# A hybrid retention / RWKV-7 / mixture-of-experts block: TensorE's order in the first phase written by the kernel

## The chip, the core and the metric

The kernel runs on one core of a Trainium2 chip. The metric is the device time of one execution in microseconds (us). Engines are named as the profile names them: PE is TensorE, PEld its weight loads, DVE VectorE, ACT ScalarE, POOL GpSimd, and SP the queue that issues almost all transfers.

## The reference

One layer over 2048 tokens of width 1024, in float32:

```python
xn = rms_norm(h, norm1_gain[l])
proj = xn @ w_in[l]
...
ret = jax.nn.silu(rp[..., 3 * RET_WIDTH:]) * ret.reshape(B, S, RET_WIDTH)
rw = rwkv7_time_mix(proj[..., 4 * RET_WIDTH:], ...)
mixed = jnp.concatenate([ret, rw], axis=-1).astype(x.dtype)
h = h + mixed @ w_out[l]
h = h + hier_moe(rms_norm(h, norm2_gain[l]), ...)
```

`ret` is retention with 4 heads of 128 (rotary q and k, decayed scores inside a chunk, a state from chunk to chunk, and a head norm). `rw` is the RWKV-7 recurrence with 8 heads of 64: each token's state is the old one times a decay, plus a rank-one correction, plus `v k^T`; then a head norm, a bonus term and a gate. The mixture of experts picks 2 of 32 experts for each token.

## The kernel before

**Phases.** The first phase makes `mixed`. The second multiplies it by `w_out` (tiles `wo`, `mT`, results `acc`) and routes the tokens. The third runs the experts. The first phase is what the change touches. Its work on TensorE falls into these parts.

- *Projections*, four groups of 512 tokens. `norm_a` and `norm_b` make the normalised, transposed input `nT` as a high and a low part; `rwkv_proj` makes 14 column blocks with 24 matmuls of 512 columns each (`gemm_fm`, results `pj`), and inside it `lora`; `ret_head` makes k, q, gate and v of one retention head (`gemm_fm`, `gemm_v`). Weights come chunk by chunk through `wchunk`: a transfer, a cast on ACT, a subtraction on DVE.
- *Retention cores* (`core`), 16 of them, one for each head and group: short products in `pk` (steps r0 to r4 below), then `head_center` (two reductions, a square, 12 small operations for the reciprocal root, on DVE, ACT and POOL in turn), then the transposes of L649.
- *RWKV units*, 16 of 128 tokens. `rwkv_prep` loads a unit, makes the norms (`pb` of 8 columns), transposes, and multiplies inner products (`pb<-ar,bk`: for each half of the unit two products whose weights and data lie on 64 partitions, the first on the lower 64, the second on the upper); their masked results are `pt`. POOL then solves 32x32 triangles in 31 double steps (L486, L488): `pt` goes to memory as `nl_d`, comes back as `ln`, the result goes out as `xl_d` and comes back as `t1s`. `rwkv_inv` joins the triangles to inverses (`psi`, beginning with the transpose of `t1s` at L511). `rwkv_chain` does two chunks of 64 tokens in series: `psr` (with the state `sbd`), `psz<-rs_,inv`, `psz<-uv,bkt` (new state), and two products `psz<-uv,pt` and `psr<-uv,pt` of 64x64. `rwkv_fin` centres the heads (`head_center`), transposes at L572 and applies the gate.

**What sets the order.** The program is written part by part. A scheduler places every instruction on its engine by a priority and by its own estimate of when operands will be ready; `tc.high_priority(offset=...)` raises a part (units `PRW`, `PRC`, `PRF`; weights `soon()`). Each engine then runs its list strictly in order, so an instruction that waits holds everything behind it.

## Time and profile before

| | us |
|---|---|
| three runs: median (lowest to highest) | 2427.48 (2424.75 to 2428.06) |
| the profiled execution: its time / its span | 2430.18 / 2428.4 |
| projections, 16 to 1188 us: length / TensorE busy | 1172.0 / 1088.2 |
| from the last projection to the first `acc`, 1188 to 1265 us | 77.0 / 54.2 |
| the rest of the second phase to the routing, 1265 to 1535 us | 270.0 / 266.3 |
| routing, 1535 to 1578 us | 43.0 / 21.6 |
| experts, 1578 to 2428 us | 850.4 / 776.9 |

The span runs from the first to the last instruction; the execution's own time is 1.8 us longer. A window's second number is the time in which at least one matmul was in flight. A matmul in flight overlaps the next, so the pace of a dense row of matmuls is read from the starts of consecutive rows and not from a mean duration.

### The profile page before, as it was taken

The page shows a single profiled execution, that of the slowest core. Times are in us where ns is not written, and L with a number is a line of the kernel's source. Part 1 is how long each engine was busy: PE and PEld are TensorE (multiplying, and loading weights), DVE is VectorE, ACT ScalarE, POOL GpSimd, SP SyncE. Part 2 cuts the span into 40 slices and gives each one's busy share as a digit, 9 for nine tenths or more (in the row PEclk, how much of TensorE's full clock was granted, in tenths as well). Part 3 has the DMA queues.
Part 4 walks back from the last instruction along what each step waited for, and adds up shares of the span by engine and source line. Part 5 has one row for each costly group of instructions (what it writes and reads, how often), then busy time and mean ns, then how long its engine had stood idle before and what let it go on. Part 6 is the DMA issues. An engine that isn't in the chain of part 4 may idle for free.

```text
span 2428.4 us, 36379 instructions
## 1 busy us (share of the span) xinstructions
PE 2207.2 (91%) x11816; PEld 1810.3 (75%) x11817; DVE 1710.4 (70%) x3500; ACT 1129.7 (47%) x1932; POOL 1161.3 (48%) x1530
## 2 busy tenths in 40 slices
PE   5999889998898989999879999699999999999990
PEld 4887778887787867877768888577777777777770
DVE  4477766878666877567775766768777787777875
ACT  4343433534434345333322222366666666666663
POOL 2036444354441575136542333466666666666650
PEclk9998999989999999999969999799999999999995
DMA  6643254432544335433234454488989999889978
GB/s 207 210 150 94 81 175 143 137 89 84 173 138 130 90 92 174 123 93 104 76 106 123 129 202 146 138 296 287 304 293 290 302 290 301 295 282 299 292 255 297
DMA packets 291298, 454.78 MB, mean 187 GB/s; under 512 B 93392, under 2 KB 164496, under 8 KB 291088
## 3 DMA queue, kind: packets, MB, share of 16 engines
q1 hardware_dynamic: 277136, 414.10, 51.6%
q0 software_dynamic: 13824, 37.80, 7.3%
q8 instruction: 94, 1.54, 0.3%
q14 instruction: 100, 0.82, 0.1%
q10 hardware_dynamic: 144, 0.52, 0.1%
HBM read 375.18 MB, written 81.85 MB: 188 GB/s over the span
## 4 chain that ended last, share of the span: by engine, by line
PE 47%; POOL 11%; DMA 7%; DVE 6%; issue 5%; ACT 3%; SPq 2%; POOLq 0%; DVEq 0%; ACTq 0%
PE acc L152 32%; PE pj L152 6%; POOL xl L488 5%; POOL tm L486 4%; PE pb L152 2%; PE tp L152 2%; ACT hl L913 1%; PE tp L1025 1%; DMA ln<-nl_d 1%; DVE hl L914 1%; PE psz L152 1%; DMA h_d<-yo,ti 1%; DMA xl_d<-xl 1%; PE psi L152 1%; SPq L490 1%
## 5 line engine op out<-in xcount | busy, mean ns | idle before, releaser
L152 PE MATMUL pj<-nT,whl 128*128 128x512 f32 x2496 | 626.4, 403 | 9.6 <-DVE nT L319 5.3
L914 DVE TENSOR_TENSOR hl<-raw,hl 128x1024 fp32r<-128x1024 f32 x259 | 444.1, 1745 | 142.6 <-ACT hl L913 142.6
L152 PEld LDWEIGHTS pj<-nT,whl 128*128 128x128 f32 x2496 | 464.9, 192 | 106.7 <-DVE nT L319 5.8
L152 PE MATMUL acc<-hl,xT 128*128 128x512 f32 (+1 forms) x2048 | 511.3, 402 | 0.0
L152 PEld LDWEIGHTS acc<-hl,xT 128*128 128x128 f32 (+1 forms) x2048 | 367.2, 183 | 100.8 <-ACT xT L172 0.2
L914 POOL TENSOR_TENSOR hl<-raw,hl 128x1024 fp32r<-128x1024 f32 x125 | 332.6, 2672 | 219.2 <-ACT hl L913 163.2
L913 ACT CAST hl<-raw 128x1024 fp32r<-128x1024 f32 x353 | 352.0, 1049 | 32.7 <-DMA raw<-in_wu_dram 26.9
L249 ACT CAST whl<-wraw 128x512 fp32r<-128x512 f32 x248 | 152.3, 618 | 304.8 <-PE pj L152 240.0
L250 DVE TENSOR_TENSOR whl<-wraw,whl 128x512 fp32r<-128x512 f32 x248 | 187.8, 760 | 146.1 <-ACT whl L249 141.7
L152 PE MATMUL acc<-hl,hT 128*128 128x512 f32 (+1 forms) x1024 | 249.6, 398 | 0.0
L486 POOL TENSOR_TENSOR tm<-xl,ln 128x60 f32<-128x60 f32 (+24 forms) x496 | 179.1, 361 | 105.6 <-DMA ln<-nl_d 69.0
L152 PEld LDWEIGHTS acc<-hl,hT 128*128 128x128 f32 (+1 forms) x1024 | 183.1, 181 | 51.7
L488 POOL TENSOR_TENSOR xl<-xl,tm 128x60 f32<-128x60 f32 (+24 forms) x496 | 187.5, 378 | 36.6
L152 PE MATMUL acc<-wo,mT 128*128 128x512 f32 x768 | 191.9, 401 | 0.0
L152 PEld LDWEIGHTS acc<-wo,mT 128*128 128x128 f32 x768 | 142.2, 191 | 28.5
L1147 POOL DMA_INDIRECT h_d<-yo,ti x48 | 107.5, 2239 | 53.8 <-DMA h_d<-yo,ti 40.5
L499 POOL COPY mbd<-pt 32x128 f32<-32x128 f32 x64 | 20.6, 321 | 226.5 <-DVE pt L464 199.4
L152 PE MATMUL pj<-whl,nT 128*128 128x256 f32 x768 | 118.6, 305 | 0.2 <-DVE gs L600 0.2
L152 PEld LDWEIGHTS pj<-whl,nT 128*128 128x128 f32 x768 | 105.9, 207 | 2.7 <-DVE gs L600 0.4
L464 DVE TENSOR_TENSOR pt<-pb,cst 64x512 f32<-64x512 f32 x128 | 88.0, 687 | 24.9 <-PE pb L152 23.1
L1014 POOL DMA_INDIRECT xb<-xt_d,ti x48 | 75.1, 1564 | 33.4 <-PE tp L1025 22.8
L172 ACT CAST xT<-tp 128x512 fp32r<-128x512 f32 x80 | 46.0, 589 | 80.7 <-PE tp L1025 65.7
(447 smaller groups left out, 3283.7 us busy)
## 6 DMA issues: line engine op xcount, KB each, us to landing
raw<-in_wg_dram SPq DMA_DIRECT2D x128, 512.0 KB, 4.7
raw<-in_wu_dram SPq DMA_DIRECT2D x128, 512.0 KB, 6.6
raw<-in_wd_dram SPq DMA_DIRECT2D x128, 512.0 KB, 6.7
wraw<-in_win_dram SPq DMA_DIRECT2D x208, 256.0 KB, 3.1
tr<-pf_d SPq DMA_DIRECT2D x80, 256.0 KB, 3.1
pf_d<-ev SPq DMA_DIRECT2D x52, 256.0 KB, 2.9
x<-in_xt_dram SPq DMA_DIRECT2D x32, 256.0 KB, 5.2
pf_d<-x SPq DMA_DIRECT2D x32, 256.0 KB, 4.2
```

The lines of the kernel that those rows point to most:

```text
L152: PE.matmul(o, l, r, start=start, stop=stop)
L172: SC.copy(dst_h, ps)
L249: SC.copy(hl[:, 0], raw)
L250: V.tensor_tensor(hl[:, 1], raw, hl[:, 0].bitcast(F32), op=ALU.subtract)
L464: V.tensor_tensor(pt[zs, i:i + 2, :, z ^ h], psp[h][zs].rearrange("p (f c) x -> p f c x", f=2), maskp[zs, None, None, :].to_broadcast([64, ...
L486: GP.tensor_tensor(tv, xl[:, 0:r, t:t + 1].to_broadcast([128, r, n]), ln[:, t:t + 1, t + 1:32].to_broadcast([128, r, n]), op=ALU.mult)
L488: GP.tensor_tensor(xl[:, 0:r, t + 1:32], xl[:, 0:r, t + 1:32], tv, op=ALU.add)
L490: SY.dma_start(xl_d[u].rearrange("l (r q) t -> q l r t", q=4)[q], xl[q * 32:(q + 1) * 32])
L913: (SC.copy if hi is SC else hi.tensor_copy)(hl[:, 0], raw)
L914: lo.tensor_tensor(hl[:, 1], raw, hl[:, 0].bitcast(F32), op=ALU.subtract)
L1014: return GP.indirect_dma_start(out=xbs[b], out_offset=None, in_=xt_d, in_offset=bass.IndirectOffsetOnAxis(ap=ti[b][:, e:e + 1], axis=0), b ...
L1147: GP.indirect_dma_start(out=h_d, out_offset=bass.IndirectOffsetOnAxis(ap=idx, axis=0), in_=y, in_offset=None, bounds_check=S + 127, comput ...
```

## The change

The first phase becomes six generators ("streams"): chains, inverses, preparations, fins, cores, projections. A clock `NOW` counts the TensorE time of what has been issued, from a formula on shape and type (0.227 for a 512-column projection matmul). `done(...)` notes it under a name in `AT`; `yield after(LAT[...], ...)` says that the stream may go on when `NOW` has come that many us past the noted point. A loop takes, at each step, the first stream in the list that may go on; if none may, it moves `NOW` ahead. TensorE's instructions stay in the order so made (`manual_schedule`); the other engines' order is still the scheduler's. Units start at least `PC_US` = 66 us apart, but for the last four.

```diff
+LAT = {"proj": 8, "load": 9, "pss": 3.5, "psi": 1.5, "bk": 11, "psp": 4.5, "pst": 1.5, "solve": 40, "i1": 1.5, "i2": 3, "inv": 3,
+       "c1": 2.5, "c2": 2.2, "c3": 3, "c4": 2, "hc": 14, "psn": 3.5, "head": 3, "r0": 2, "r1": 2.5, "r2": 4, "r3": 2, "r4": 15}
+PC_US = 66.0
...
+    NOW = [0.0]
+
     def mm(o, l, r, start=True, stop=True):
+        n = math.prod(r.shape[1:])
+        NOW[0] += max(0.107, n * 0.000443) if r.dtype == F32R else 2 * max(0.057 if r.shape[0] <= 64 else 0.107, n * 0.00088)
         PE.matmul(o, l, r, start=start, stop=stop)
+
+    def flip(o, i, ident_):
+        NOW[0] += 0.11
+        PE.transpose(o, i, ident_)
...
+        AT, INF, LOCK = {}, 1e9, [None]
+
+        def done(*k):
+            AT[k] = NOW[0]
+
+        def after(lag, *keys):
+            return lambda: max(AT.get(k, INF) for k in keys) + lag
...
         def gemm_fm(i, nT):
             ps = pj.tile([128, 512], F32, name="pj")
             for kh in range(2):
                 hl = wchunk(A["win"][i, :, kh * 512:(kh + 1) * 512])
                 for k in range(4):
+                    yield
...
+            done("load", u)
+            yield after(LAT["load"], ("load", u))
...
+            done("pss", u)
+            yield lambda: max(AT["pss", u] + LAT["pss"], AT.get(("chain", u - 2), INF if u > 1 else 0.0),
+                              AT.get(("fin", u - 3), INF if u > 2 else 0.0), PACE(u))
+            ar = rp.tile([128, 4, 2, 128], F32, name="ar", bufs=2)
...
-            psb = pb.tile([128, 4, 128], F32, name="pb")
-            mm(psb.rearrange("p f t -> p (f t)"), blk2, rt)
-            V.tensor_tensor(bon, psb, f3(vt), op=ALU.mult)
+            done("psi", u)
+            yield after(LAT["psi"], ("psi", u))
...
+            done("psv", u)
+            yield after(LAT["bk"], ("psi", u))
...
-                pst = pb.tile([128, 2, 2, 128], F32, name="pb")
-                for q in range(4):
-                    PE.transpose(pst[:, q % 2, q // 2], bk[:, i * 2 + q], ident)
-                SC.copy(bkt[:, :, i * 128:(i + 2) * 128], pst.rearrange("p c f x -> p c (f x)"))
-
+                done("psp", u, i)
+                yield after(LAT["psp"], ("psp", u, i))
...
+            done("solve", u)
+            for i in range(0, 4, 2):
+                pst = pb.tile([128, 2, 2, 128], F32, name="pb")
+                for q in range(4):
+                    flip(pst[:, q % 2, q // 2], bk[:, i * 2 + q], ident)
+                SC.copy(bkt[:, :, i * 128:(i + 2) * 128], pst.rearrange("p c f x -> p c (f x)"))
+                done("pst", u, i)
+                yield after(LAT["pst"], ("pst", u, i))
+            psb = pb.tile([128, 4, 128], F32, name="pb")
+            mm(psb.rearrange("p f t -> p (f t)"), blk2, rt)
+            V.tensor_tensor(bon, psb, f3(vt), op=ALU.mult)
+            done("prep", u)
...
+            yield lambda: INF if LOCK[0] else AT["solve", u] + LAT["solve"]
+            LOCK[0] = u
...
+            yield lambda: max(AT.get(("pst", u, 2), INF) + LAT["pst"], AT.get(("fin", u - 2), INF if u > 1 else 0.0))
...
+                done("c1", u, c)
+                yield lambda: max(AT["c1", u, c] + LAT["c1"], AT.get(("inv", u), INF) + LAT["inv"])
...
+                done("c2", u, c)
+                yield after(LAT["c2"], ("c2", u, c))
...
-            head_center(yt, 8, 64, 64e-5, py.tile([128, 512], F32, name="psi"))
+            head_center(yt, 8, 64, 64e-5, sm.tile([128, 512], F32, name="sqf", bufs=1))
+            done("hc", u)
+            yield lambda: INF if LOCK[0] is not None else AT["hc", u] + LAT["hc"]
...
+                if h == 3 and g + 1 < NG:
+                    norm_b(g + 1)
...
-            head_center(y, 4, 128, 1e-5, pk.tile([128, 512], F32, name=pkn))
-            psn = pk.tile([128, 512], F32, name=pkn)
+            head_center(y, 4, 128, 1e-5, pkb.tile([128, 512], F32, name="pk"))
+            done("r", j, 4)
...
+        def PACE(u):
+            return AT["proj", 0] + PC_US * u if u < NU - 4 else 0.0
...
+        streams = [(each(rwkv_chain, NU), PRC), (each(rwkv_inv, NU), PRC), (each(rwkv_prep, NU), PRW),
+                   (each(rwkv_fin, NU), PRF), (each(core, 4 * NG), PRO), (projections(), None)]
+        with tc.manual_schedule(engines={mybir.EngineType.PE}):
+            ready = [next(s) for s, _ in streams]
+            while any(s for s, _ in streams):
+                times = [(r() if callable(r) else 0.0 if s else INF) if s else INF for (s, _), r in zip(streams, ready)]
+                if min(times) >= INF:
+                    raise RuntimeError(f"no stream can go on: {AT}")
+                NOW[0] = max(NOW[0], min(times))
+                i = next(i for i, t in enumerate(times) if t <= NOW[0])
+                s, pri = streams[i]
+                with (tc.high_priority(offset=pri) if pri else ExitStack()):
+                    try:
+                        ready[i] = next(s)
+                    except StopIteration:
+                        streams[i] = (None, None)
     ga.close()
```

The rest of the diff puts `done` and `yield after` with the lags of `LAT` behind every further step (c3, c4, i1 to i2, psn, r0 to r3), splits `norm_b` so that its scaling is issued ahead of the group's last gate product, moves a scratch tile of the fin from PSUM to SBUF and gives the last core the same PSUM pool as the others. The number of instructions and their shapes stay as they are.

Three places in TensorE's order, before and after. First the inner products of unit 7 (`pb<-ar,bk`; the numbers tell the two results of a half apart). Before:

```order
L152 MATMUL pb_5070<-ar_4987,bk_5040 128x128 x4
L152 MATMUL pk_6376<-vtm_6032,rc_6356 128x128 x4
L152 MATMUL pj_6810<-nT3_6434,whl_6813 128x512 x3
L152 MATMUL pj_6810<-nT4_6438,whl_6830 128x512 x3
L152 MATMUL pj_6810<-nT5_6442,whl_6830 128x512 x3
L152 MATMUL pj_6810<-nT6_6446,whl_6830 128x512 x3
L152 MATMUL pj_6810<-nT7_6450,whl_6830 128x512 x3
L152 MATMUL pj_6851<-nT0_6422,whl_6854 128x512 x2
L511 MATMUL psi_4844<-cst_119,t1s_4833 128x128
L152 MATMUL pj_6851<-nT0_6422,whl_6854 128x512
L152 MATMUL pj_6851<-nT1_6426,whl_6854 128x512 x3
L152 MATMUL pb_5071<-ar_4987,bk_5040 128x128 x4
```

After:

```order
L160 MATMUL pb_6683<-ar_6551,bk_6568 128x128
L160 MATMUL pb_6684<-ar_6551,bk_6568 128x128
L160 MATMUL pb_6683<-ar_6551,bk_6568 128x128
L160 MATMUL pb_6684<-ar_6551,bk_6568 128x128
L160 MATMUL pb_6683<-ar_6551,bk_6568 128x128
L160 MATMUL pb_6684<-ar_6551,bk_6568 128x128
L160 MATMUL pb_6683<-ar_6551,bk_6568 128x128
L160 MATMUL pb_6684<-ar_6551,bk_6568 128x128
L160 MATMUL psz_6697<-uv_5753,bkt_5752 128x128 x4
```

The two products of a half stood 4 to a row with other work between them; now they alternate, one on the lower 64 partitions and one on the upper. It is so in all 32 halves (before, one half alternates throughout and a few for some rows), and in the same way the two 64x64 products of all 32 chunks alternate, which none did.

Second, the first chunk of unit 7's chain, from the product with the inverse (`psz<-rs_`) to the new state (`psz<-uv,bkt`). Before:

```order
L152 MATMUL psz_7387<-rs__7382,inv1_148 128x64 x4
L152 MATMUL pb_7180<-ar_7097,bk_7150 128x128 x4
L152 MATMUL pj_8659<-whl_8691,nT3_6434 128x256 x3
L152 MATMUL pj_8658<-whl_8720,nT4_6438 128x256 x3
L152 MATMUL pj_8658<-whl_8720,nT5_6442 128x256 x3
L152 MATMUL pj_8658<-whl_8720,nT4_6438 128x256 x3
L152 MATMUL pj_8658<-whl_8720,nT5_6442 128x256 x3
L152 MATMUL pj_8659<-whl_8720,nT4_6438 128x256 x3
L152 MATMUL pj_8659<-whl_8720,nT5_6442 128x256 x3
L152 MATMUL psz_7394<-uv_4990,bkt_4989 128x128 x4
```

After:

```order
L160 MATMUL psz_7384<-rs__6975,inv1_148 128x64 x4
L164 MATMUL pb_7391<-cst_119,tr_7199 128x128 x4
L160 MATMUL pj_7315<-whl_7381,nT2_5706 128x256 x3
L160 MATMUL pj_7315<-whl_7381,nT3_5709 128x256 x3
L160 MATMUL pj_7315<-whl_7381,nT2_5706 128x256 x3
L160 MATMUL pj_7315<-whl_7381,nT3_5709 128x256 x3
L160 MATMUL pj_7316<-whl_7381,nT2_5706 128x256 x3
L160 MATMUL pj_7316<-whl_7381,nT3_5709 128x256 x3
L160 MATMUL psz_7420<-uv_6554,bkt_6553 128x128 x4
```

There were 21 projection matmuls of 256 columns and a group of four inner products between the two; now there are 18 matmuls and four transposes.

Third, the end of the phase. Before, the last rows ahead of the first `acc`:

```order
L572 MATMUL psi_10903<-cst_119,yt_10572 128x128 x4
L152 MATMUL psi_10912<-lg_8180,lw_135 128x128 x4
L152 MATMUL psr_11309<-uv_10646,pt_10644 64x64 x4
L152 MATMUL psr_11320<-uv_10646,pt_10644 128x128 x4
L152 MATMUL psr_11320<-sbd_143,ar_10643 128x128 x4
L649 MATMUL pj_12887<-cst_119,rc_12854 128x128 x4
L152 MATMUL psz_11333<-rs__11329,inv1_148 128x64 x4
L152 MATMUL pb_11430<-tr_11371,cst_119 128x512
L447 MATMUL pb_11433<-cst_119,tr_11372 128x128 x4
L152 MATMUL acc_13059<-wo7_12982,mT_13049 128x512
```

After:

```order
L160 MATMUL psi_12496<-lg_11141,lw_135 128x128 x4
L164 MATMUL psi_12503<-cst_119,t1s_12222 128x128
L160 MATMUL pb_12506<-ar_12421,bk_12438 128x128
L160 MATMUL pb_12507<-ar_12421,bk_12438 128x128
L160 MATMUL pb_12506<-ar_12421,bk_12438 128x128
L160 MATMUL pb_12507<-ar_12421,bk_12438 128x128
L160 MATMUL pb_12506<-ar_12421,bk_12438 128x128
L160 MATMUL pb_12507<-ar_12421,bk_12438 128x128
L160 MATMUL pb_12506<-ar_12421,bk_12438 128x128
L160 MATMUL pb_12507<-ar_12421,bk_12438 128x128
L160 MATMUL psi_12503<-t1s_12222,mbd_151 128x32 x4
L160 MATMUL acc_13062<-wo7_12985,mT_13052 128x512
```

Before, the first `acc` stood behind a part of unit 15's preparation and 19 rows ahead of unit 14's inverse; now it stands behind the inner products of unit 15 and behind the first two steps of unit 14's inverse (`psi<-cst,t1s`, `psi<-t1s,mbd`). The last projection row stands 56 rows above it.

## Rows read from the trace of the kernel before

**Rows 1.** The page: span, TensorE's busy time, and its two strips of 40 slices.
```profile
span 2428.4 us, 36379 instructions
PE 2207.2 (91%) x11816; PEld 1810.3 (75%) x11817; DVE 1710.4 (70%) x3500; ACT 1129.7 (47%) x1932; POOL 1161.3 (48%) x1530
...
PE   5999889998898989999879999699999999999990
...
PEclk9998999989999999999969999799999999999995
```
**Rows 2.** Windows by stage: length, busy time of each engine, granted clock, DMA share.
```profile
16.00:1188.00 1172.00, 1088.22 (x6293) 919.01 (x6293) 827.58 (x1881) 467.59 (x954) 493.70 (x1043) 0.96 0.42 126
1188.00:1265.00 77.00, 54.19 (x297) 47.34 (x296) 57.87 (x152) 28.73 (x61) 42.97 (x97) 0.68 0.37 106
1265.00:1535.00 270.00, 266.31 (x1546) 227.79 (x1544) 167.69 (x679) 74.91 (x177) 94.29 (x151) 0.99 0.47 147
1535.00:1578.00 43.00, 21.55 (x99) 17.56 (x100) 29.53 (x119) 14.87 (x19) 16.62 (x13) 0.64 0.43 141
1578.00:2428.40 850.40, 776.90 (x3587) 598.65 (x3585) 624.31 (x650) 537.13 (x705) 508.77 (x216) 0.96 0.89 292
```
**Rows 3.** Waits of TensorE, 0 to 1500 us: total, times, longest.
```profile
PE psi L511 <- DMA t1s<-xl_d: 42.4, 16, 4.8
...
PE pk L152 <- ACT rc L621: 8.9, 3, 4.9
PE pb L152 <- DVE tr L441: 6.7, 7, 1.8
...
PE pj L152 <- ACT x L339: 4.8, 10, 1.4
...
PE pk L649 <- POOL rc L379: 3.9, 2, 3.4
...
PE psz L152 <- ACT uv L546: 0.8, 1, 0.8
```
**Rows 4.** Timeline of one solve (unit 4): start, length, engine, line, operation.
```profile
457.88 1.38 DVE L464 TENSOR_TENSOR pt<-pb,cst 64x512 f32<-64x512 f32 x2
459.29 0.80 SPq L474 DMA_DIRECT2D nl_d<-pt  x2
461.34 1.71 SPq L481 DMA_DIRECT2D ln<-nl_d  x4
465.64 0.24 POOL L486 TENSOR_TENSOR tm<-xl,ln 128x31 f32<-128x31 f32 x1 [5.70 <-DMA ln<-nl_d]
...
501.12 0.21 POOL L488 TENSOR_TENSOR xl<-xl,tm 128x8 f32<-128x8 f32 x1
501.35 2.52 SPq L490 DMA_DIRECT2D xl_d<-xl  x4
505.24 1.95 SPq L503 DMA_DIRECT2D t1s<-xl_d  x4
508.67 0.30 PE L511 MATMUL psi<-cst,t1s 128*128 128x128 f32 x1 [2.11 <-DMA t1s<-xl_d]
```
**Rows 5.** Windows around the end of that solve.
```profile
504.00:509.00 5.00, 2.89 (x18) 2.36 (x16) 3.46 (x4) 1.10 (x2) 1.56 (x1) 1.00 0.26 40
509.00:523.00 14.00, 14.00 (x64) 13.33 (x65) 5.05 (x10) 1.68 (x4) 1.14 (x4) 0.51 0.38 103
```
**Rows 6.** The chain that ended last: a stretch of 512-column matmuls without a wait.
```profile
1411.05 11.92 PE acc L152 x52
```
**Rows 7.** Timeline of TensorE: inner products of 64 rows, apart and interleaved.
```profile
764.96 1.16 PE L152 MATMUL pb<-ar,bk 64*128 64x128 f32 x8
766.05 2.18 PE L152 MATMUL pj<-whl,nT 128*128 128x256 f32 x16
...
775.17 1.16 PE L152 MATMUL pb<-ar,bk 64*128 64x128 f32 x16
776.26 1.16 PE L152 MATMUL pk<-qT,kT 128*128 128x128 f32 x8
...
1204.40 0.68 PE L152 MATMUL psr<-uv,pt 64*64 64x64 f32 x8
1205.00 1.16 PE L152 MATMUL pk<-rc,qT 128*128 128x128 f32 x8
1206.09 0.68 PE L152 MATMUL psz<-uv,pt 64*64 64x64 f32 x8
1206.69 1.16 PE L152 MATMUL psr<-uv,pt 128*128 128x128 f32 x8
```
**Rows 8.** Timeline of TensorE: last projection, an inverse, first output product.
```profile
1186.30 2.08 PE L152 MATMUL pj<-nT,whl 128*128 128x512 f32 x8
...
1214.33 0.45 PE L511 MATMUL psi<-cst,t1s 128*128 128x128 f32 x1 [3.61 <-DMA t1s<-xl_d]
...
1265.31 3.29 PE L152 MATMUL acc<-wo,mT 128*128 128x512 f32 x10
```
**Rows 9.** Timeline: a chunk's second product, and the ends of two head-centre steps.
```profile
462.99 1.08 PE L152 MATMUL psz<-rs__4237,inv 128*128 128x64 f32 x8
464.11 0.42 DVE L545 COPY uv<-psz 64x256 f32<-64x256 f32 x1 [0.54 <-PE psz L152]
464.56 0.37 ACT L546 COPY uv<-psz 64x256 f32<-64x256 f32 x1 [0.28 <-DVE uv L545]
...
468.75 1.05 PE L152 MATMUL psz<-uv,bkt 128*128 128x128 f32 x8
...
478.61 1.16 PE L152 MATMUL pk<-vtm,rc 128*128 128x128 f32 x8
...
499.67 1.49 POOL L379 TENSOR_TENSOR rc<-rc,rs_y 128x512 f32<-128x512 f32 x1
...
1240.76 1.91 PE L152 MATMUL pj<-vtm,rc 128*128 128x128 f32 x8
...
1258.37 1.04 POOL L379 TENSOR_TENSOR rc<-rc,rs_y 128x512 f32<-128x512 f32 x1
```

201 lines of the change are left out of this document (114 added, 87 removed).

## The prediction

> **What bounds the kernel now.** I read the page first, then the kernel by stages, then who waited for whom on the engine that is busiest. TensorE has something in flight for 91% of the span, and its strip stays at 8 or 9 but for two dents [rows 1]. The stages tell where the rest lies [rows 2]. In the projections, 16 to 1188 us, matmuls are in flight for 1088 of 1172 us: 84 us are idle. The granted clock there is 0.96, so about 0.04 x 1172 = 47 us of full-speed work are lost as well. In the stretch from the last projection to the first output product, 54 of 77 us are busy, at a clock of 0.68. The rest of the second phase is dense (266 of 270). Routing and experts, 893 us, are not touched.
>
> Nearly half of the idle time is one wait: the transpose that begins a unit's inverse waits for `t1s`, 16 times, 42.4 us together, 4.8 at most [rows 3]. Unit 4 shows what is behind it: the last masked product is done at 459.3, the triangles go to memory and come back, POOL solves from 465.6 to 501.3, the result goes out and comes back, and the transpose starts at 508.7 [rows 4]. That is 49 us, in which only rows of other work keep TensorE busy. [...] So TensorE is the bound of the first phase, and order alone can win back at most some 84 + 47 us there, and part of the 77.
>
> **The change, part by part.** All counts are of rows in the order, with paces from the trace: 0.229 us for a projection matmul of 512 columns (52 in 11.92 us) [rows 6], about 1.0 us for a group of four short float32 matmuls, and 0.6 us for the four of 64x64 [rows 7].
>
> *Pairs.* Four inner products on one half of the partitions, 8 passes, take 1.09 us to the next instruction (764.96 to 766.05). The one place where the two halves alternate has 16 passes in the same 1.09 us (775.17 to 776.26) [rows 7]. The change alternates all 32, of which one did: 31 x 1.09 = 34 us; I take 33 for those that did so in part. It lies on TensorE's path, nothing hides it. For the 64x64 products no alternating place exists. Apart, 8 passes take 0.60 us (1204.40 to 1205.00), 0.075 each [rows 7]; the alternating inner products run at 0.068 a pass, and at that pace 16 passes take 1.09 instead of 1.20: 32 x 0.11 = 4 us, which I take because it is the nearest row. If they overlapped fully it would be 32 x 0.60 = 19, if not at all 0. [...]
>
> *The inverse's distance.* Between the last inner product of unit 7 and its inverse stood 136 projection matmuls (31 us), six groups of short matmuls (6) and a few transposes and small ones (2): 39 us. Now there are 156 (36), seven groups (7) and 3 more: 46. Over units 0 to 13 the same count gives 42 us on average before and 46 after. The mean wait was 42.4 / 16 = 2.65 us, less than the 4 us that are added. But time between passes faster if the clock stays up and pairs overlap, and the solve itself has no reason to be quicker. I take 25 of the 42 us; the ends are 0 and 42.
>
> *The clock.* If most inverses no longer wait, most of the drops that follow them go too. Of the 47 us I take 20, less than the share of the waits, since other waits may bring the clock down; ends 0 and 47.
>
> *The end of the phase.* From the last projection to the first output product stood 32 us of rows in 77 us. Now there are 21 us of rows, but the first output product is queued behind unit 14's inverse, and that unit's inner products end only 4 us of rows ahead of the last projection. By unit 4 [rows 4], 50 us lie between the products and the inverse, so the first output product starts 50 - 4 + 2 = 48 us or so after the last projection. Rows not covered: 77 - 32 = 45 before, 48 - 21 = 27 after; with the weights of the output product loading in that time too I take 16 of the 18. Ends: 0 and 25. In [rows 8] the inverse of unit 13 stands in the middle of that stretch and waits 3.6.
>
> *Small things.* The bonus product moves from before to behind the solve, so its operand is old when it comes: it waited 6.7 us in 7 waits. Other streams go between the `lora` products, which waited 4.8 for ACT [rows 3]. I take 8 of 11.5. What else moves costs nothing while its lead lasts: the transposes of `bk` with their copies on ACT go behind the solve's transfers, the load of `lg` goes behind the norms and, in SP's list, behind the unit's other loads, and `norm_b`'s eight multiplications go ahead of a gate product. Their users (the new state, the fin's gate, the next group) stand ten us of rows or more behind them; without that lead each would be a wait of a few us once in a unit or group.
>
> *What it adds.* The scheduler left more room behind short steps than the lags do. From the product with the inverse to the new state the median was 5.0 us of rows and is now 2.5. In the trace the copies between them were done 0.9 us after the product's end, with 4.7 us until the next (464.07, 464.93, 468.75) [rows 9], so 2.5 is enough there, unless DVE is late; the row of `uv` in [rows 3] shows 0.8 us in all. The tight place is a core's head centring: 19 us of rows before, 16 after. In the trace it took from 479.8 to 501.2, 21.4 us, in one core, and from 1242.7 to 1259.4, 16.7 us, in another [rows 9]; before, the transposes waited only 3.9 us for it in all [rows 3], as other delays fell into the same 19 us. By these two the shortfall is 1 to 5.5 us in each of 16 cores, 16 to 88. A fin's head centring, with 16 us now where some 90 stood, can fall short in the same way. Behind such a transpose the whole list of TensorE waits, projections too. I take 55 for all of them, as waits elsewhere in the same 16 us cover part; ends 15 and 90.
>
> Sum: -33 - 4 - 25 - 20 - 16 - 8 + 55 = -51. The profiled execution took 2430.2, its span 2428.4 [rows 1]; 2430.2 - 51 = 2379. The median of the runs was 2.7 below the profiled execution, so I predict 2376.
>
> **The rivals.**
>
> *Slower: head centring becomes the wait that the inverse was.* Every core falls short by the 5.5 us of the slower row, 88 us, and each such wait brings the clock down as in [rows 5]: at the 47 / 16 = 3 us that a unit loses now, 48 us more, and nothing of the 20 is won. -33 - 4 - 25 - 16 - 8 + 88 + 48 = +50: 2478. It decides from a mean wait of some 4 us with such a clock, or 6.6 without. For it: 21.4 against 16, and that its DVE operations stand at low priority. Against it: waits share their time, and the same arithmetic for the order before would give waits that [rows 3] doesn't show. [...] Here the trace shows a fall after a single wait [rows 5], and no run here shows yet what many short ones do.
>
> *No change: the inverse waits as long as before.* POOL's list is still the scheduler's; if it puts rope and fin work among the solve's steps, the solve grows by what the distance has grown. Already now the last step of unit 4's solve came behind a head-centre product of POOL (499.67, then 501.12) [rows 4, 9]. Without the 25 and the 20: -6, 2421.
>
> *Much faster: the lags fit.* The head centrings cost 15, inverses and clock give back 40 each, the end of the phase 20: -37 - 40 - 40 - 20 - 10 + 15 = -132, 2295. For it: the short steps have the room that [rows 9] asks.
>
> **How the numbers follow.** The forecast has a chance of 0.50 (its own range 2345 to 2405), much faster 0.15, no gain 0.13, slower 0.22. A measurement of this kernel can tell about 0.2%, 5 us. Faster: 0.50 + 0.15 + half of the third = 0.71; same 0.07; slower 0.22. The range that leaves out 2 in 10, half of the best case and the far part of the slower one: 2310 to 2455.
>
> **What would show it.** The alternating inner products stand as rows of 16 passes with 1.1 us to the next instruction. The total of waits for `t1s` falls below 20 us. The clock of the projection window is 0.98 or more. The window from the last projection to the first output product is near 50 us. Waits for POOL's head-centre products at the two transposes total 30 to 60 us. The prediction is wrong if those pass 90, if the waits for `t1s` stay above 35, or if the projections are held by something that has no row here, as late weights.

## The result, and the profile after

The changed kernel takes 2492.4 us (median of 4 runs, 2489.8 to 2498.5) against 2427.8 before: a ratio of 1.0266, interval 1.0236 to 1.0296. I had forecast 2376. The profiled execution took 2498.5, its span 2496.8.

The page's span, TensorE's busy time and its two strips, to be read beside [rows 1]:

```profile
span 2496.8 us, 36285 instructions
...
PE 2171.8 (87%) x11816; PEld 1780.9 (71%) x11817; DVE 1719.3 (69%) x3500; ACT 1133.7 (45%) x1932; POOL 1136.2 (46%) x1530
...
PE   5998789886898887898967999699999999999990
...
PEclk9999889999899998899987999799999999999995
```

TensorE is busy for 35 us less in a span that is 68 us longer, and the clock's strip has 8s where it had 9s. The windows by stage (last projection now at 1284, first output product at 1345, last at 1594), with the columns of [rows 2]:

```profile
16.00:1284.00 1268.00, 1092.22 (x6489) 923.51 (x6490) 867.44 (x1979) 482.54 (x981) 486.02 (x1087) 0.92 0.40 119
1284.00:1345.00 61.00, 29.23 (x202) 25.16 (x200) 42.66 (x106) 21.67 (x43) 32.49 (x72) 0.69 0.40 115
1345.00:1594.00 249.00, 248.04 (x1437) 213.16 (x1436) 149.88 (x615) 67.95 (x159) 85.25 (x128) 0.99 0.49 153
```

Against [rows 2] the projections take 96 us more, the stretch to the first output product 16 less, the output products 21 less; what follows takes 903 us against 893, which stays unexplained (this execution was the longest of the four). A part of that is work that changed its place: 196 more matmuls stand in the first window and 204 fewer in the two behind it. Over all three together it is 59 us more.

The loss lies in the projections. TensorE is idle there for 176 of 1268 us (84 of 1172 before). By the clock's own records in the two traces it is busy for 152 us (76 before) at a granted share of 0.5. In such a stretch of the changed kernel's trace six projection matmuls of 512 columns take 2.71 us (1118.81 to 1121.52), 0.45 each, where 512-column matmuls take 0.229 in [rows 6]; so I put the loss at half of those times, 76 us (38 before). That is 92 + 38 = 130 us more. It came to 96, although more matmuls stand there, since the rows themselves got shorter: 1092 - 76 = 1016 us of full-speed work against 1088 - 38 = 1050. (One minus the clock of the row, times the length, gives more, 101 against 47, because it also counts time in which TensorE was idle; the prediction's 47 was read so.)

Who ended TensorE's waits, 0 to 1600 us, as in [rows 3] (total, times, longest):

```profile
PE psr L160 <- DVE yt L624: 30.3, 16, 7.7
PE pk L160 <- DVE srt L730: 27.4, 7, 6.7
PE pk L164 <- POOL rc L410: 25.1, 6, 7.1
PE psi L164 <- POOL yt L410: 22.1, 4, 9.3
PE psi L160 <- DVE wbd L569: 16.7, 6, 7.2
...
PE pj L160 <- DVE nT L351: 14.1, 4, 5.8
PE pj L160 <- ACT x L372: 10.6, 11, 2.2
PE pk L164 <- DVE rc L752: 8.1, 8, 2.1
PE psi L160 <- DVE t1s L562: 8.0, 4, 2.8
PE psi L164 <- DVE inv L576: 7.2, 2, 4.0
...
PE psz L160 <- ACT uv L605: 4.9, 5, 2.2
PE pk L160 <- ACT rc L738: 4.2, 1, 4.2
```

The first row of [rows 3], 42.4 us that the inverse waited for `t1s`, is gone. In its place stands a dozen short waits, most of them for VectorE (DVE). One of them, the longest on `psr`, seen on TensorE and on VectorE (start, length):

```profile
261.95 0.22 PE L160 MATMUL psr<-uv,pt 64*64 64x64 f32 x1
269.86 1.44 PE L160 MATMUL psr<-uv,pt 128*128 128x128 f32 x5 [7.69 <-DVE yt L624]
```

```profile
262.15 1.00 DVE L408 TENSOR_SCALAR hv<-hv 128x4 f32<-128x4 f32 x1
...
263.66 5.22 DVE L342 TENSOR_TENSOR x<-x,ev 128x512 f32<-128x512 f32 x5
...
269.06 0.42 DVE L624 TENSOR_TENSOR yt<-yt,psz 64x256 f32<-64x256 f32 x1
269.40 0.41 DVE L624 TENSOR_TENSOR yt<-yt,psr 64x256 f32<-64x256 f32 x1
```

This wait shows the loss in small. A unit's last 64x64 products end at 262.2. The next unit's first product comes right behind them in TensorE's list and needs the same PSUM buffer `psr`, of which there is one; it is free when VectorE has added it to `yt`. VectorE is not slow: those two rows take 0.8 us. It is busy from 262 to 269 with other rows, five of them `norm_b`'s multiplications, which the change moved ahead. TensorE, whose order is fixed, waits for all of them, though it has projections to do. Around it the granted clock falls:

```profile
255.00:262.00 7.00, 5.19 (x44) 4.20 (x42) 6.13 (x12) 1.72 (x3) 4.67 (x10) 1.00 0.17 32
262.00:270.00 8.00, 0.31 (x7) 0.17 (x3) 7.90 (x13) 0.72 (x1) 5.50 (x5) 0.63 0.73 179
270.00:284.00 14.00, 12.42 (x57) 10.57 (x57) 13.19 (x39) 8.24 (x14) 3.13 (x3) 0.85 0.11 34
```

The third window is what the wait costs besides itself: the mean clock of 0.85 stands for some 4 us at a share of 0.5 (by the records it holds from 264.0 to 274.3), which lose 0.15 x 14 = 2 us of full-speed work.

The pairs (the alternating products) did what was meant, and more. TensorE's timeline, to be read beside [rows 7]:

```profile
1143.96 1.16 PE L160 MATMUL pb<-ar,bk 64*128 64x128 f32 x16
1145.05 1.10 PE L160 MATMUL psz<-rs__10717,inv 128*128 128x64 f32 x8
...
1153.19 0.27 PE L160 MATMUL psz<-uv,pt 64*64 64x64 f32 x1
1153.20 0.27 PE L160 MATMUL psr<-uv,pt 64*64 64x64 f32 x1
...
1153.80 0.97 PE L160 MATMUL pj<-nT,whl 128*128 128x512 f32 x3
```

16 passes of the inner products take 1.09 us, as many as 8 took alone. 16 passes of 64x64 take 0.61 us (1153.19 to 1153.80), where 8 took 0.60.

### The profile page after: what moved, and what is told of

It is laid out like the page before. It is cut to its first block, busy times and chain, and to the rows that moved or that the text cites. A ratio compares the mean times of both kernels' runs of the same rounds, so it can differ in the third digit from the quotient of the medians.

```text
span 2496.8 us, 36285 instructions
## 1 busy us (share of the span) xinstructions
PE 2171.8 (87%) x11816; PEld 1780.9 (71%) x11817; DVE 1719.3 (69%) x3500; ACT 1133.7 (45%) x1932; POOL 1136.2 (46%) x1530
## 4 chain that ended last, share of the span: by engine, by line
PE 42%; DVE 7%; issue 5%; POOL 4%; DMA 4%; ACT 2%; SPq 1%; DVEq 0%; POOLq 0%; ACTq 0%
PE acc L160 29%; PE pj L160 5%; POOL xl L523 2%; POOL tm L521 2%; PE tp L160 1%; PE tp L1129 1%; ACT hl L1017 1%; DVE hl L1018 1%; DVE pt L501 1%; DMA h_d<-yo,ti 1%; DMA ln<-nl_d 1%; DMA hl<-h_d 1%; PE psz L160 1%; PE psr L160 1%; PE psi L160 1%
## 5 line engine op out<-in xcount | busy, mean ns | idle before, releaser
L160 PE MATMUL pj<-nT,whl 128*128 128x512 f32 x2496 | 655.1, 414 | 22.8 <-DVE nT L351 14.1
L160 PEld LDWEIGHTS pj<-nT,whl 128*128 128x128 f32 x2496 | 478.1, 198 | 125.1 <-DVE nT L351 16.7
L262 DVE TENSOR_TENSOR whl<-wraw,whl 128x512 fp32r<-128x512 f32 x248 | 178.7, 723 | 162.9 <-ACT whl L261 159.7
L521 POOL TENSOR_TENSOR tm<-xl,ln 128x60 f32<-128x60 f32 (+24 forms) x496 | 165.7, 334 | 107.1 <-DMA ln<-nl_d 70.4
L523 POOL TENSOR_TENSOR xl<-xl,tm 128x60 f32<-128x60 f32 (+24 forms) x496 | 172.8, 348 | 36.8
L160 PE MATMUL pj<-whl,nT 128*128 128x256 f32 x768 | 110.9, 301 | 2.7 <-DVE gs L689 2.7
L472 POOL TENSOR_TENSOR tr<-tr 128x512 f32<-128x512 f32 x16 | 21.8, 1363 | 174.9 <-ACT tr L471 174.9
```

Of the source, the lines that this page charges most:

```text
L160: PE.matmul(o, l, r, start=start, stop=stop)
L262: V.tensor_tensor(hl[:, 1], raw, hl[:, 0].bitcast(F32), op=ALU.subtract)
L472: GP.tensor_tensor(kt, kt, ta, op=ALU.mult)
L521: GP.tensor_tensor(tv, xl[:, 0:r, t:t + 1].to_broadcast([128, r, n]), ln[:, t:t + 1, t + 1:32].to_broadcast([128, r, n]), op=ALU.mult)
L523: GP.tensor_tensor(xl[:, 0:r, t + 1:32], xl[:, 0:r, t + 1:32], tv, op=ALU.add)
```

## Experiments

All eighteen are timed beside the kernel before on their own chip; the ratio is to that. Chips differ by a few us (the kernel before took 2424.6 to 2435.0 on them), so small differences between runs of two chips are better read from the ratios. The last three columns are of the window from 16 us to the last projection: its length, TensorE's idle time in it, its granted clock. The windows do not hold quite the same work: 6293 matmuls in the kernel before, 5752 in before_pairs, 6335 in before_light, 6392 to 6491 in all others.

| run | us | ratio, interval | length | idle | clock |
|---|---|---|---|---|---|
| kernel before | 2427.8 | 1 | 1172 | 84 | 0.96 |
| changed kernel | 2492.4 | 1.0266 (1.0236 to 1.0296) | 1268 | 176 | 0.92 |
| short_lags | 2519.2 | 1.0393 (1.0361 to 1.0425) | 1272 | 189 | 0.92 |
| long_centring | 2504.0 | 1.0337 (1.0294 to 1.0379) | 1266 | 182 | 0.93 |
| long_both | 2511.5 | 1.0346 (1.0321 to 1.0372) | 1267 | 183 | 0.92 |
| core_priority | 2487.2 | 1.0261 (1.0229 to 1.0293) | 1255 | 167 | 0.93 |
| priorities | 2495.0 | 1.0273 (1.0242 to 1.0304) | 1262 | 172 | 0.92 |
| vector_order | 2589.2 | 1.0679 (1.0623 to 1.0734) | 1334 | 216 | 0.89 |
| pairs_apart | 2501.7 | 1.0322 (1.0291 to 1.0354) | 1271 | 155 | 0.92 |
| before_pairs | 2583.9 | 1.0637 (1.0616 to 1.0659) | 1056 | 78 | 0.97 |
| light_vector | 2435.9 | 1.0029 (1.0009 to 1.0049) | 1205 | 135 | 0.94 |
| before_light | 2406.1 | 0.9900 (0.9874 to 0.9926) | 1148 | 68 | 0.97 |
| counted_queue | 2487.2 | 1.0229 (1.0174 to 1.0284) | 1249 | 170 | 0.93 |
| counted_longer | 2525.0 | 1.0380 (1.0325 to 1.0434) | 1270 | 183 | 0.91 |
| buffer_release | 2470.9 | 1.0186 (1.0144 to 1.0227) | 1242 | 160 | 0.93 |
| counted_release | 2434.0 | 1.0038 (1.0014 to 1.0061) | 1189 | 133 | 0.95 |
| counted_short | 2426.6 | 0.9996 (0.9976 to 1.0015) | 1183 | 121 | 0.94 |
| centring_both | 2470.6 | 1.0159 (1.0133 to 1.0185) | 1213 | 142 | 0.93 |
| centring_first | 2468.0 | 1.0147 (1.0118 to 1.0175) | 1215 | 140 | 0.93 |
| centring_cores | 2469.1 | 1.0147 (1.0124 to 1.0170) | 1217 | 139 | 0.92 |

**Are the distances too short?** This was the first theory (A), from the prediction's own words: the distances are shorter than the steps take. Its rival (B) was the order of VectorE's list. short_lags makes those behind the short steps longer:

```diff
-LAT = {"proj": 8, "load": 9, "pss": 3.5, "psi": 1.5, "bk": 11, "psp": 4.5, "pst": 1.5, "solve": 40, "i1": 1.5, "i2": 3, "inv": 3,
-       "c1": 2.5, "c2": 2.2, "c3": 3, "c4": 2, "hc": 14, "psn": 3.5, "head": 3, "r0": 2, "r1": 2.5, "r2": 4, "r3": 2, "r4": 15}
+LAT = {"proj": 8, "load": 9, "pss": 5, "psi": 3, "bk": 11, "psp": 4.5, "pst": 1.5, "solve": 40, "i1": 4, "i2": 5.5, "inv": 4.5,
+       "c1": 5, "c2": 4.5, "c3": 5.5, "c4": 4, "hc": 14, "psn": 4.5, "head": 3, "r0": 4.5, "r1": 5, "r2": 7, "r3": 4.5, "r4": 15}
```

> The changed kernel, with the distances behind its short steps made longer (c1, c2, c3, i1, i2, r1, r2 and their like by 1.5 to 3 us each); head centring, solve, pairs and all else stay. Theory A (the new waits stand because the distances are about the median of what the steps take on VectorE and ScalarE, so that every second one is late): the waits for the state of the cores (27.4 us), for yt of the chain (30.3), for wbd, t1s and the inverse (33.1), for uv, rs_ and the other results on rc (about 20) fall from some 110 us together to under 50, the clock of the projections rises from 0.92 towards 0.95, and the time falls by 60 to 90 us, to 2400 to 2430. Theory B (the order on VectorE and GpSimd, which the scheduler still makes, puts these steps behind other work whenever they stand): they are as late at the longer distance, and the time falls by less than 20 us.

long_centring sets only `hc` and `r4`, from 14 and 15 to 24.

> The changed kernel, with the two distances behind head centring longer: 14 to 24 us for a unit, 15 to 24 us for a core; all else stays. Theory A (the distances are shorter than the steps take): the waits for GpSimd's last product of head centring, 25.1 and 22.1 us, fall below 10 together, the clock comes up a little, and the time falls by 35 to 55 us, to 2437 to 2457. Theory B (GpSimd puts head centring among the steps of the solve, so that it comes as late whatever the distance): it falls by under 15 us. If the slower rival of the prediction were the whole cause, the time would come down to that of the kernel before.

long_both has both edits.

> The changed kernel with both sets of distances longer, those behind the short steps and those behind head centring. Theory A (each set moved the waits to the other, since both are short): together the waits in the projections fall by more than half and the time by 60 us or more, below 2430. Theory B (VectorE's list is behind, and a step comes late wherever it stands, because the rows ahead of it are late too): the waits move again and the time stays between 2480 and 2530.

All three are slower than the changed kernel. Each set did away with some of the waits that it was aimed at and found others. In short_lags the cores' wait for `srt` fell from 27.4 to 8.8 us, but the one for `yt` rose from 30.3 to 34.8 and head centring's from 47.2 to 70.5. In long_centring the waits for head centring no longer stand among the first, and these do:

```profile
PE psi L160 <- DVE wbd L569: 42.3, 11, 9.2
PE pk L164 <- DVE rc L752: 23.6, 12, 4.2
```

In long_both the inverse waits for its solve again, and buffers are waited for as before:

```profile
PE psi L164 <- DMA t1s<-xl_d: 41.0, 8, 8.5
PE psr L160 <- DVE yt L624: 29.7, 13, 7.1
PE pk L164 <- DVE rc L752: 17.7, 10, 4.8
```

So theory A falls as it stood: distances that are longer everywhere do not help. My reading, which no run shows by itself, is that a wait that goes also takes away the time that it gave to all that was under way.

**Is it the order of the other engines' lists?** core_priority raises the cores from 0 to 9000; priorities sets chain and inverse to 12000, cores and fins to 9000, the preparation to 3000 and the weights' splits to 0.

> The changed kernel, with the priority of the cores' work on VectorE, ScalarE and GpSimd at 9000 instead of 0; TensorE's order is the same row for row. Theory B (the scheduler's order on VectorE is what makes the steps late): the waits for the state of the cores (27.4 us), their head centring (25.1) and their last products (8.1 and 4.2) fall by more than half, the others grow by less, and the time falls by 25 to 45 us. Theory A (the distances): what the cores win, the steps of chain and inverse lose, as VectorE has the same work in the same order of TensorE; the time changes by under 15 us.

> The changed kernel with other priorities for the scheduler's lists: the chain's and the inverse's rows ahead of all (12000), those of the cores and of the units' ends 9000, the units' preparation 3000, the weights' splits 0; TensorE's order stays but for some places. If the priorities of the lists on VectorE make the steps late, the time falls by 40 us or more. If the scheduler's lists follow the times at which it thinks rows are ready, and priorities decide little (as with the cores' alone), the time stays within 15 us of 2490.

Neither moved the time by what a measurement can tell. vector_order writes VectorE's list out by the same plan:

```diff
-        with tc.manual_schedule(engines={mybir.EngineType.PE}):
+        with tc.manual_schedule(engines={mybir.EngineType.PE, mybir.EngineType.DVE}):
```

with the steps split as its expectation says.

> The changed kernel with VectorE's list in the first phase written out by the same plan as TensorE's, no longer the scheduler's: a step's rows for VectorE stand right behind those of the steps that TensorE was given before. So that they don't wait at the head of the list, rows that need another engine first are put off (a projection's evacuation by two steps of the next one, the second half of head centring by 6 us, bk's second half by 6.5 us behind its transposes, the scan by 10 us behind its loads), and weights are split two chunks ahead. Theory B (the steps are late because the scheduler's list for VectorE puts other rows ahead of them): the waits for VectorE fall by half or more, from 112 us in the projections, and the time falls by 50 to 110 us, to 2380 to 2440. If it is VectorE's load as such and not its order: within 25 us of 2492. If waiting at the head of a written list is worse: above 2520.

It is the slowest of all, 97 us above the changed kernel. VectorE then waits 233 us at the head of its list for ScalarE's half of the weights' split (160 in the changed kernel), and TensorE is idle for 216. So this written order is worse than the scheduler's; whether a better one exists was not tried. What speaks against theory B is that no priority moved the time.

**What are the pairs worth?** pairs_apart changes the loops back to one half of the partitions behind the other:

```diff
-                for q in range(4):
-                    for h in range(2):
+                for h in range(2):
+                    for q in range(4):
...
-                for f in range(4):
-                    for h in range(2):
+                for h in range(2):
+                    for f in range(4):
```

> The changed kernel, with the pairs of products on one half of the partitions each one behind the other instead of alternating, in the inner products and in the products of 64x64; the distances and the rest of the order stay. If pairs overlap as the trace of the changed kernel shows (16 passes of 64x64 in 0.6 us, 16 of the inner products in 1.1), the time grows by 33 us for the inner products and 19 for the 64x64, to about 2544. If time given to TensorE there is lost in the waits behind (the steps that follow come later too), it grows by 15 to 30 us.

It costs 9 us by the medians and 14 by the ratios, not 52, and less than the 15 to 30 of the other forecast. But the edit does not take 52 us back. Two groups of which one stands right behind the other still overlap in part:

```profile
1147.00 1.71 PE L160 MATMUL pb<-ar,bk 64*128 64x128 f32 x16
1148.64 1.10 PE L160 MATMUL psz<-rs__10717,inv 128*128 128x64 f32 x8
...
1156.15 0.50 PE L160 MATMUL psz<-uv,pt 64*64 64x64 f32 x5
1156.44 0.27 PE L160 MATMUL psr<-uv,pt 64*64 64x64 f32 x1
1156.49 0.22 PE L160 MATMUL psz<-uv,pt 64*64 64x64 f32 x1
...
1157.05 0.96 PE L160 MATMUL pj<-nT,whl 128*128 128x512 f32 x3
```

16 passes of the inner products take 1.64 us so (1.09 alternating, twice 1.09 if nothing overlapped), 16 of 64x64 take 0.90 (0.61, and twice 0.60). That adds 32 x 0.55 + 32 x 0.29 = 27 us to TensorE's rows. The window of its projections, beside the first of the changed kernel:

```profile
16.00:1287.00 1271.00, 1116.37 (x6489) 950.28 (x6490) 870.92 (x1981) 482.01 (x981) 484.96 (x1089) 0.92 0.39 118
```

TensorE is busy for 24 us more and idle for 21 less. The stretch is 3 us longer. With its order fixed, most of what TensorE's rows win there is lost again in the waits behind them. What the whole 52 us are worth no run shows. The other way round, before_pairs binds the pairs in the scheduler's order (each product queued behind the one of the other half):

```diff
+        if prev is not None:
+            tc.add_manual_dep(ins.ins, prev.ins.name, mybir.DependencyInfo(
+                mybir.DependencyClass.NoSync, mybir.DependencyReason.DATA), reason="pairs")
```

> The kernel before, whose TensorE order stays the scheduler's, with one part of the change alone: the products of each pair are bound in alternating order, inner products and 64x64 alike. If TensorE's rows bound that kernel, it wins what the pairs overlap: 31 x 1.09 + 32 x 0.60 = 53 us by the rows of the changed kernel, at most, less if the scheduler's order moves for the worse: 2370 to 2385. If that phase is no longer bound by TensorE once its rows are shorter (as putting the pairs apart in the changed kernel cost 9 us of 52), it wins 10 to 20: 2405 to 2415.

It came out on neither side: 156 us slower. Its windows of projections and of the output products:

```profile
16.00:1072.00 1056.00, 977.69 (x5752) 826.56 (x5753) 746.20 (x1666) 429.86 (x856) 396.53 (x802) 0.97 0.43 131
...
1142.00:1675.00 533.00, 385.77 (x2149) 325.97 (x2149) 258.34 (x882) 117.15 (x276) 182.66 (x410) 0.78 0.30 91
```

The projections ran ahead and were done 116 us earlier than before, at an idle time of 78. The units were left behind, and the output products took 533 us instead of 270, between their steps. A pair needs both of two PSUM buffers at once, which units get less often than one; that this is what held them back I only argue. The run says nothing on what pairs are worth.

**Is it VectorE's load?** light_vector takes one kind of row off VectorE, before_light does the same to the kernel before. Both leave out the lower half of the projection weights (ScalarE writes zeros in its place), so they only probe the load:

```diff
-                V.tensor_tensor(hl[:, 1], raw, hl[:, 0].bitcast(F32), op=ALU.subtract)
+                SC.activation(hl[:, 1], raw, AF.Copy, scale=0.0)
```

> The changed kernel with VectorE relieved of one row kind: the lower half of each projection weight is written as zeros by ScalarE (some 0.6 us a row) and not subtracted on VectorE (248 rows of 0.72 us, 179 us, with another 160 us in which VectorE waits at their head for ScalarE). Matmuls, transfers and TensorE's planned order stay. Theory B (TensorE waits for rows that are queued on a busy VectorE): the waits for VectorE fall by more than half, the clock of the projections rises, and the time falls by 60 to 110 us, to 2380 to 2430. Theory A (distances too short for the steps themselves, not for the queue): it falls by less than 25 us.

> The control: the kernel before with the same relief of VectorE (the lower half of each projection weight written as zeros by ScalarE). There TensorE waits for VectorE for some 20 us in the projections and for the solve's result for 42. Theory B: the scheduler's order already stands around VectorE's load, so the time falls by 5 to 25 us only, to 2400 to 2420. If VectorE bounds both kernels alike, both fall by the same amount.

The changed kernel wins 56 us, the kernel before 22. TensorE's waits for VectorE in the window of projections, without the one at the start, fell from 119 to 80 us: by a third, less than the half that theory B asked for, as the time fell by a little less than its 60. So some 34 of the 65 us that the change lost hang on those rows; the rest stays with VectorE at 708 instead of 867 us of work in that window. The edit does two things at once: it takes the work off VectorE, and with it the 160 us in which VectorE stood at the head of these rows waiting for ScalarE. No run parts the two. ScalarE has 127 us more to do (609 against 483).

**What does the plan not count?** Theory C: VectorE's queue. A wrapper around VectorE's operations adds up what the plan has given it, and a step's distance begins where that is worked off:

```diff
+                VQ[0] += 0.15 + 0.00104 * n
...
         def done(*k):
-            AT[k] = NOW[0]
+            AT[k] = NOW[0] + BEHIND[0]
...
+                BEHIND[0] = max(0.0, VQ[0] - NOW[0])
```

> The changed kernel, whose plan now counts VectorE's queue as well: every VectorE row adds 0.15 us and 1.04 ns for each column (from the traces: 0.68 us for 512 columns, 0.28 for 128), and a step's distance begins where VectorE would have worked off what it was given before. The distances themselves stay; lists of the other engines stay the scheduler's. Theory C (fixed distances are met on the average but not behind VectorE's bursts, and the scheduler's order knew these bursts): the waits in the projections fall by a third or more, from 187 us, and the time falls by 40 to 90 us, to 2400 to 2450. If it goes as with the longer fixed distances (each wait that goes comes back at another step), it stays between 2480 and 2530.

> The same with head centring's distances at 18 and 21 us instead of 14 and 15 and the solve's at 42 instead of 40, as GpSimd's queue is not counted. Theory C: the waits for GpSimd's last product of head centring (47 us in the changed kernel) fall below 20 and the time by another 10 to 30 us against the run beside it. Else: no more than 10 us of difference.

The first gained 5 us (9 by the ratios), the second lost 33. But now the waits that are left show their kind. Those of counted_queue (through the wrapper VectorE's rows all have line 151):

```profile
PE psr L173 <- DVE yt L151: 49.6, 15, 8.2
PE psi L177 <- DVE inv L151: 34.2, 12, 5.3
PE pk L177 <- POOL rc L425: 20.1, 3, 10.6
...
PE pk L177 <- DVE rc L151: 13.9, 8, 4.5
```

The waits for `srt` and `wbd`, 44 us in the changed kernel, are down to 2. Three of the four rows are waits for a PSUM buffer of which there is one: `psr` from a unit to the next, `psi` from the inverse's copies to the fin's transposes, `pk` from a core to the next. The plan has no distance for those. Theory D: the plan counts what a row reads, not which buffer it must find free.

```diff
+       "psy": 2, "psw": 2.5, "psm": 2, "psf": 1.5, "pkf": 2}
...
-            yield after(LAT["head"], ("head", j))
+            yield lambda: max(AT.get(("head", j), INF) + LAT["head"], AT.get(("core", j - 1), INF if j else 0.0) + LAT["pkf"])
```

and the same for the chain's start (`psy`) and each next tile `psi` (`psw`, `psm`, `psf`).

> The changed kernel with distances also behind the release of PSUM buffers of which there is one: 2 us from a unit's last products on psr to the next unit's first, 1.5 to 2.5 us before the next tile psi of inverse or fin, 2 us from a core's last product to the next core's transposes. Theory D (the plan counts what a row reads and not which buffer it has to find free): the waits for yt on psr (30.3), the inverse's copies (7.2) and the last product on rc (8.1) fall from 46 to under 20 us, and the time by 20 to 45 us, to 2447 to 2472. Else (what goes here comes back elsewhere): within 12 us of 2492.

> Both: VectorE's queue counted and the distances behind the buffers' release. Theories C and D together (queue and buffers are what the scheduler's order knew and the plan did not): the waits in the projections fall from 187 us to under 110, the half clock with them, and the time falls to 2390 to 2450. If a fixed order loses to the chip's own spread whatever the plan counts: 2470 or more.

> The same with the distances of chain, inverse and cores cut to the steps' own durations (c1 1.5, c2 1.5, c3 2.2, i1 1, i2 2.2, r0 1.2, r1 1.5, r2 2.5, r3 1.5 us), as the queue is counted now, and with the lora products behind their projection's evacuation, so that they have two PSUM buffers and not one. If the longer recurrence is what counting costs, it gains 10 to 30 us against counted_release; if the short distances fall short again, it loses as much. The waits for the lora results (some 10 us) fall below 5.

Buffers alone win 22 us, queue and buffers together 58: 2434, inside the forecast range, though TensorE's waits in the projections fell from 192 to 148 us only and not under 110. The buffers' waits are nearly gone in counted_release, and the two largest that are left are the solve's and head centring's, whose distances count neither GpSimd's queue nor the transfers' (behind them come two of 19 us for VectorE, on `gs` and `nT`):

```profile
PE psi L178 <- DMA t1s<-xl_d: 34.7, 7, 8.9
PE pk L178 <- POOL rc L426: 31.2, 7, 9.6
...
PE psr L174 <- DVE yt L152: 6.0, 3, 4.3
```

counted_short, with the distances cut to what the steps take, won 7 us more and stands level with the kernel before (the `lora` part of it did nothing: 8.8 us of waits). Both theories hold, but they need each other: alone, queue and buffers won 5 and 22 us, together 58; with the queue alone the waits went to the buffers.

**The last waits.** In counted_short two rows are left above all:

```profile
PE psi L178 <- POOL yt L426: 36.4, 5, 14.1
PE pk L178 <- POOL rc L426: 28.2, 6, 11.1
```

centring_both sets head centring's distances to 20 and the solve's to 36; centring_first adds priorities of 12000 for both; centring_cores leaves the units' at 14.

> counted_short with the distances behind head centring at 20 us for units and cores (14 and 15) and the solve's at 36 (40), since its result lay 19 us on the average. If the waits left are those of a distance that counts no GpSimd: the two waits for its last product fall from 65 to under 25 us, others grow by 10 at most, and the time falls by 25 to 50 us, to 2377 to 2402, faster than both kernels. If a unit's end that is put off delays the chains and inverses behind it, as in counted_longer: 2420 to 2450.

> The same with the priorities of units' ends and cores at 12000, ahead of the preparation's 10000, so that head centring's products may stand ahead of the solve's on GpSimd. If that list makes them late: their waits fall by 10 us or more against the run beside it and the time by 5 to 20 us. If the lists follow the times at which rows become ready, as with the priorities tried before: within 6 us of it.

> counted_short with the cores' distance alone at 20 us and the solve's at 36; the units' stays at 14. If units' ends may not be put off: faster than centring_both by 5 us or more. If they may: slower by 10 to 30 us, the waits for the units' product stay at 30 us or more, those for the cores' fall below 12.

All three lose some 40 us against counted_short, alike. They share two edits that I should have kept apart: the solve's 36 and the cores' 20. Head centring's waits did fall, from 65 to 14 us in centring_both, and in centring_cores the units' part of them fell from 36.4 to 0.5 although its distance stayed at 14. But in centring_both:

```profile
PE psi L178 <- DMA t1s<-xl_d: 51.7, 8, 10.1
...
PE pk L178 <- POOL rc L426: 13.8, 3, 5.1
```

In counted_short GpSimd's last step of a solve lay 19 us on the average before the inverse, but in unit 13 only 7, which is the time of its transfers (7.3 in [rows 4]), and the inverse waited 1.7 us in all. That the 4 us taken off this distance brought the 52 us back is the nearest reading, but not shown: in counted_release the same wait stood at 34.7 us with the distance at 40, and in long_both at 41.0. What longer head centring alone would give in this plan was not run, and no version here that does all of the work beats the kernel before.

## Why the prediction was wrong, point by point

*Pairs (-33 and -4): rows right and one too small, the path wrong.* The inner products went as [rows 7] said, 31 x 1.09. The 64x64 products overlap in full, 16 passes in 0.61 us: 19, not 4. The two halves start 0.01 us apart (1153.19 and 1153.20). My nearest row was one of products that overlap in another shape. The step that failed is "it lies on TensorE's path, nothing hides it": pairs_apart gives 27 of these 52 us back to TensorE's rows, and 9 to 14 of the 27 reach the end of the kernel; in the projections 21 us of idle time went for 24 of work.

*The inverse's distance (-25): right, and larger.* The 42.4 us went entirely, and more than the 4 us of rows that I counted had a part in it. On the mean of the 16 units 16.5 us now lie between GpSimd's last step of the solve and TensorE's transpose (8.0 in unit 11, 27.7 in unit 1); before it was 7.5, and 7.3 in [rows 4]. The distance from the last inner products to the transpose grew by 7.4 us, from 50.4 to 57.8, and the solve itself, which I had said had no reason to be quicker, became 2.3 us shorter (32.3 to 30.0). That the distance grew by more than my 4 us because other rows' waits now fall into it is likely, but no run shows it. The lead is not safe: counted_release, with the same 40 in its plan, has 34.7 us of this wait again, counted_short 1.7.

*What it adds (+55): this step failed.* It priced head centring, and that was close: 25.1 + 22.1 = 47 us, within the 30 to 60 that I gave for it. It priced everything else that stands closer at nothing: "2.5 is enough there, unless DVE is late", from one chunk of [rows 9] in which VectorE was free. VectorE was late. The waits for `yt`, `srt`, `wbd`, `t1s`'s copy, `inv`, the last product on `rc`, `uv` and ACT's `rc` make 107 us, where the kernel before had 22: 8.9 and 0.8 in [rows 3], 1.6 for `inv`, 1.1 for `rc`, and

```profile
PE psr L152 <- ACT yt L540: 6.3, 2, 5.7
...
PE psr L152 <- DVE yt L561: 3.0, 4, 1.2
```

What the runs showed in its place is that the plan leaves out two things that these steps meet: the rows ahead on VectorE's list, and the release of a PSUM buffer. Counting both takes 58 of the 65 us back. That the scheduler's order had both in it is the plain reading of that, but no run shows it directly.

*The clock (-20): wrong sign, by the same step.* 38 us more were lost, not 20 won: TensorE waited more, and the time at a granted share of 0.5 in the projections went from 89 to 191 us (76 and 152 of them busy). The clock of the projections roughly follows TensorE's idle time over the runs of the table: 0.97 at 68 us, 0.95 at 133, 0.92 at 176, 0.89 at 216.

*The end of the phase (-16): the number came out by luck.* The window went from 77 to 61 us, but because 95 fewer matmuls stand in it, which moved ahead into the projections and cost there. TensorE's idle time in it did not fall by the 18 us of uncovered time that I had worked out; it rose from 23 to 32. The first output product stands 61 us behind the last projection and not 48, since unit 14's inverse began 62 us behind its inner products and not 50.

*Small things (-8): wrong.* `lora` waits 10.6 instead of 4.8, the bonus product's 6.7 went, and "what else moves costs nothing while its lead lasts" looked at the rows' own users: `norm_b`'s multiplications had theirs far behind, but 5.2 us of them stood in front of a `yt` that was waited for.

*The rivals.* The slower one came within 14 us of the time, with a clock that lost 38 us more where it said 48, but named the wrong place: head centring cost 47 and not 88; short steps and buffers cost the rest. "The inverse waits as long as before" and "the lags fit" are both refuted.

## What to carry to other kernels

When a scheduler's order is replaced by one from fixed rules, every wait that the rules don't know can come back (here 107 us, where the order before had 22): ask of each step not only how long its work takes, but what stands ahead of it on the other engine's list, and which buffer the next step must find free. Price a step by the worst of its rows and not by a free moment, and take nothing from an average lead whose least value is already used up. Shorter rows need not bring the end forward on an engine that waits for others in a fixed order: between pairs_apart and the changed kernel 24 us of TensorE's rows moved its idle time by 21 us and the end of the projections by 3.

## What the runs showed of the hardware that was not expected

Four 64x64 float32 products on one half of the partitions and four on the other, into two buffers, take 0.61 us for 16 passes, with 8 alone at 0.60: the second half adds 0.01 us.

They need not alternate for a part of that. In pairs_apart the products of the second half stand behind all those of the first, and 16 passes take 0.90 us (1.64 for the inner products, with 8 alone at 1.09). By its trace the second half's first pass starts at 1156.44, ahead of the last three of the first half (1156.49 to 1156.61).
